# Two-layer decoder trunk on one core: norm factors spread by products, later norm sums, and another order in the first mixer

## The chip, the core and the metric

The kernel runs on one core of one Trainium2 chip. The metric is the device time of one execution in microseconds (us); lower is better. Five engines work side by side and meet at semaphores: TensorE (PE in the profile, its weight loads PEld), VectorE (DVE), ScalarE (ACT), GpSimd (POOL) and SyncE (SP), which here only issues the loads of weights. TensorE writes to eight PSUM banks; everything else lies in SBUF.

## What is computed

```python
def reference(...):                        # x: (1, 256, 1024) float32, two layers
    h = x
    for layer in range(2):
        h = h + 0.5 * swiglu(rms_norm(h, ffn1_norm[layer]), ...)     # FFN of width 2816
        hn = rms_norm(h, mix_norm[layer])
        if layer % 2 == 0:
            h = h + ab_mixer(hn, ab_w_in[0], ab_v_norm[0], ab_w_spatial[0], ab_b_spatial[0], ab_w_out[0])
        else:
            h = h + c_mixer(hn, c_w_in[0], c_w_out[0])
        h = h + 0.5 * swiglu(rms_norm(h, ffn2_norm[layer]), ...)
    return rms_norm(h, final_norm)
```

- `rms_norm(x, g)` is `x * rsqrt(mean(x*x) + 1e-6) * g`, `swiglu` is `(silu(x @ w_gate) * (x @ w_up)) @ w_down`.
- `ab_mixer` projects `hn` to q, k, v of 8 heads of 64 (attention with three dilated windows, which for 256 positions is one causal attention with a count mask) and to u and v of 4 groups of 128: `gelu(u) * (tril(w_s) @ rms_norm(gelu(v)) + b_s)`. Both results, side by side, go through `ab_w_out`.
- `c_mixer` is causal attention of 16 heads of 64 (with 256 positions there is one block only), then `c_w_out`.

## The kernel before

**Layout.** The residual `X` lies transposed: 8 tiles of 128 features by 256 positions. All products are made in three passes, `mm3` (L224 to L226): each operand is split into a rounded part and a rest (names ending in h and l, or `whi` and `wlo`), and hi x hi, lo x hi, hi x lo are added in a PSUM bank.

**Weights.** `Stream` loads them in a fixed list of pieces of 1 MB or less (`raw`, three buffers, SP queue). Each piece is split by ScalarE (L105, `whi`) and VectorE (L106, `wlo`), in two halves of 128x1024, into one of four buffers. A piece's buffer comes free when TensorE has used it (`free`), and the next split follows. A piece marked `reset` has another layout: its first three row blocks are stored as halves elsewhere, and it is split in three cuts (128x384 twice, 128x1280).

**Norms.** The next phase begins on features that are not yet divided by the root of the mean square. `Next.pair` adds a phase's result to `X`, makes the operands `xTh`, `xTl`, and squares; `acc` (L283 to L289, VectorE) adds the squares. `sums` (L295) adds them over features with two products with a column of ones, VectorE adds epsilon (L297, `ms`), GpSimd takes the power -0.5 (L233, `rstd`). `spread` (L310 to L317) brings the factor of a position to all 128 partitions: ScalarE writes `wide`, the factor of each position along a row; TensorE transposes it in two steps of 128x128 (L313); ScalarE copies the bank to `row` and half of it to `half`. An FFN calls `sums` after its second tile and `spread` after its third.

**Mixers.** A tile of projected features is 24 matmuls of 256 columns (`tiles`, two to a piece). `token_block` makes 512 columns of v, positions in the partitions: four steps of 12 matmuls of 512 columns. After each step `Slots.step` runs the work entered for that slot: `scores` of one head (four matmuls; then the row maximum on VectorE, Exp on ScalarE, the scaling by 1/sum, which the first mixer does on ScalarE, L688, and the second on GpSimd, L690), `turn` (three transposes L698, split into `pth` on ScalarE and `ptl` on VectorE), `weighted` (six matmuls with v for a pair of heads, split into `mixh` and `mixl`), and in the first mixer `mixing` of one gating group (two FP32 products, L839, then VectorE and a split). `put_q`, `put_k`, `put_u`, `put_v`, `keep_g` take a bank away: q and k need `row` (VectorE), ScalarE and GpSimd; u and g need Gelu on ScalarE (L857, L822).

`first_tiles` makes the first two q tiles and the first two k tiles (slots 0 to 3) in four banks, calls `sums` between them and `spread` behind them, and then takes the four banks away.

The first mixer's order is q and k of heads 0 to 3, v (slots 4 to 7), g (8 to 11), u (12 to 15), q and k of heads 4 to 7 (16 to 19), then `project` (20 on), which takes the eight parts of the concatenated result in the order `MIX1`: gating groups first. The order of the instructions of each engine's queue comes from a scheduler that starts from this order; each engine runs its queue strictly in order. ScalarE reads its functions from a table; the program holds a load (`ACT_TABLE_LOAD`) wherever the next function is not in the loaded one. Copies and squares do not change it, while Exp, Gelu and Silu each do.

Of the kernel before, what the change touches and what calls it, by code (L numbers as in the profile page):

```python
# [10 lines left out]
F32 = mybir.dt.float32  # L11
F32R = mybir.dt.float32r
AF = mybir.ActivationFunctionType
ALU = mybir.AluOpType
# [3 lines left out]
NT = S // 128  # L18
KD = D // 128
# [4 lines left out]
SCALE = HD ** -0.5  # L24
# [118 lines left out]
def trunk(ctx: ExitStack, tc: tile.TileContext, a, out):  # L143
# [40 lines left out]
        for c in (0, 512):  # L184
            st.add(m[k * 128 : (k + 4) * 128, c : c + 512], 4, 512, SHIFT)

    MIX1, MIX2 = (4, 5, 6, 7, 0, 1, 2, 3), (0, 1, 2, 3, 4, 5, 6, 7)
    add_ffn(a["ffn1_w_gate"][0], a["ffn1_w_up"][0], a["ffn1_w_down"][0], again=(1, 3))
    wab = a["ab_w_in"][0]
    add_cols(wab, 0, 256)  # L190
    add_cols(wab, 512, 256, reset=RESET)
    add_cols(wab, 1024, 512)
    add_cols(wab, 2048, 512)
    for c, n in ((1536, RESET), (1792, 0), (256, RESET), (768, RESET)):
        add_cols(wab, c, 256, reset=n)
    add_mix(a["ab_w_out"][0], MIX1)
    add_ffn(a["ffn2_w_gate"][0], a["ffn2_w_up"][0], a["ffn2_w_down"][0])
    add_ffn(a["ffn1_w_gate"][1], a["ffn1_w_up"][1], a["ffn1_w_down"][1])
    wc = a["c_w_in"][0]
    for c in range(4):  # L200
        add_cols(wc, c * 256, 256, reset=RESET if c % 2 else 0)
        add_cols(wc, 1024 + c * 256, 256, reset=0 if c else RESET)
        if c % 2 == 0:
            add_cols(wc, 2048 + c * 256, 512)
    add_mix(a["c_w_out"][0], MIX2)
    add_ffn(a["ffn2_w_gate"][1], a["ffn2_w_up"][1], a["ffn2_w_down"][1], True, (2, 3, 7))


# [36 lines left out]
    class Next:  # L245
# [59 lines left out]
        def spread(self):  # L305

            y = norm["col"]
            b = wk.tile([128, NT, 128], F32, name="wide", bufs=1)
            for t in range(NT):
                nc.scalar.activation(b[:, t], ones, AF.Copy, scale=y[:, t : t + 1])  # L310
            p = bank()
            for t in range(NT):
                nc.tensor.transpose(p[:, t * 128 : (t + 1) * 128], b[:, t], ident)  # L313
# [435 lines left out]
            step()  # L749
        st.free()  # L750

    def first_tiles(put_q, put_k, step):

        ps4 = [bank() for _ in range(4)]
        w = st.take()
        for j, ks in LATE:
            tile_of(ps4[j], w, j, ks)
        for _ in range(2):
            step()
        st.free()  # L760
        nxt.sums()
        w = st.take()
        for j in range(2):
            tile_of(ps4[2 + j], w, j)
            step()
        nxt.spread()
        norm["score"] = wk.tile([128, NT], F32, name="score", bufs=1)
        nc.vector.tensor_scalar(norm["score"], norm["col"], -SCALE, None, op0=ALU.mult)
        for j in range(2):
            put_q(j, ps4[j])  # L770
            put_k(j, ps4[2 + j])
        st.free()


    def token_block(evict, step):
# [20 lines left out]
    def ab_mixer(phase):  # L796
        with tc.tile_pool(name="mp", bufs=1) as mp:
            mix = mix_tiles(mp)
            v = v_tiles(mp, 512)
            vn = mp.tile([128, NT, 512], F32, name="vn")  # L800
            uT = mp.tile([128, 4, S], F32, name="uT")
            put_q, put_k, scores, turn, weighted = make_attention(mp, slice(0, 384), 8, v, mix, nc.scalar)

            vgain = mp.tile([128, 512], F32, name="vgain")
            nc.scalar.dma_start(vgain, rows(a["ab_v_norm"][0], 512))
            wsp = mp.tile([128, 4, 128], F32, name="wsp")
            nc.scalar.dma_start(wsp, a["ab_w_spatial"][0].rearrange("g p q -> p g q"))
# [12 lines left out]
            def keep_g(t, p):  # L820
                g = mp.tile([128, 512], F32, name="gv")
                nc.scalar.activation(g, p, AF.Gelu_apprx_tanh, scale=norm["col"][:, t : t + 1])  # L822
                ss = wk.tile([128, 4], F32, name="ssg")
                for q in range(4):
                    nc.scalar.activation(vn[:, t, q * 128 : (q + 1) * 128], g[:, q * 128 : (q + 1) * 128], AF.Square,
                                         accum_out=ss[:, q : q + 1])
                m = wk.tile([128, 4], F32, name="msg")
                nc.vector.tensor_scalar(m, ss, 1.0 / 128, EPS, op0=ALU.mult, op1=ALU.add)
                y = wk.tile([128, 4], F32, name="rsg")
                rsqrt(y, m, 4)  # L830
                for q in range(4):
                    cs = slice(q * 128, (q + 1) * 128)
                    nc.vector.scalar_tensor_tensor(vn[:, t, cs], g[:, cs], y[:, q : q + 1], vgain[:, cs],
                                                   op0=ALU.mult, op1=ALU.mult)

            def mixing(g):
                p = bank()
                for t in range(NT):
                    nc.tensor.matmul(p[:, t * 128 : (t + 1) * 128], vn[:, t, g * 128 : (g + 1) * 128],  # L839
                                     wsT[:, g, :], start=True, stop=True)  # L840
# [12 lines left out]
            slots.at((13, 14, 24, 25), weighted)  # L853

            def put_u(i, p):
                nc.vector.tensor_mul(uT[:, i, :], p[:, :S], norm["row"])
                nc.scalar.activation(uT[:, i, :], uT[:, i, :], AF.Gelu_apprx_tanh)  # L857

            step = slots.step
            first_tiles(put_q, put_k, step)  # L860
            token_block(lambda t, p: put_v(v, t, p), step)
            token_block(keep_g, step)
            for put, c in ((put_u, 0), (put_u, 1), (put_q, 1), (put_k, 1)):
                tiles(put, c, step)
            project(mix, MIX1, phase, step)
            assert not slots.events


    def c_mixer(phase):
        with tc.tile_pool(name="mp", bufs=1) as mp:  # L870
            mix = mix_tiles(mp)
            v = v_tiles(mp, D)
            put_q, put_k, scores, turn, weighted = make_attention(mp, slice(384, 768), 16, v, mix, nc.gpsimd, True)

            slots = Slots()
            slots.at((5, 6, 7, 8, 12, 13, 14, 15, 16, 17, 18, 19, 24, 24, 25, 25), scores)
            slots.at((8, 9, 10, 11, 15, 16, 17, 18, 19, 20, 21, 22, 26, 26, 27, 27), turn)
            slots.at((11, 13, 18, 20, 22, 24, 28, 29), weighted)
            step = slots.step
            for c in range(4):  # L880
                if c:
                    tiles(put_q, c, step)
                    tiles(put_k, c, step)
                else:
                    first_tiles(put_q, put_k, step)
                if c % 2 == 0:
                    token_block(lambda t, p: put_v(v, t, p, c * 256), step)
            project(mix, MIX2, phase, step)
            assert not slots.events


# [46 lines left out]
```

## Time and profile before

| | before |
|---|---|
| time, median of 3 runs | 948.4 us (948.16 to 948.5) |
| profiled execution, its own time | 948.47 us |
| its span, first to last instruction | 946.7 us |
| granted TensorE clock, mean | 0.999 |
| instructions | 18120 |
| first mixer, first to last of its matmuls on TensorE | about 190 to 284.6 us |
| second mixer, the same | about 646 to 764 us |
| weights and inputs read | 172.65 MB |

How to read it: a busy share is that of the whole span. Matmuls overlap, so TensorE's busy share counts the time in which any of them is under way; what it loses is seen in the distance from one start to the next. In a list of groups, the last column is the idle time of the engine just ahead of these instructions, and who ended most of it. In a list of waits, the numbers are the total in us, how many, and the longest. In a timeline the first two numbers are the start and the duration in us. In a table of windows the columns are the window, its length, and the busy time (with the number of instructions) of PE, PEld, DVE, ACT and POOL, then the clock, the share of the DMA engines and GB/s.

### The profile page before, as it was taken

The numbers are of one execution on the slowest core, as the hardware profiler recorded it, in microseconds if no ns is written. First come the engines' busy times: TensorE is split into PE (matmuls) and PEld (weight loads), VectorE is DVE, ScalarE is ACT, GpSimd is POOL, SyncE is SP. The second block draws the span as 40 slices with busy tenths as digits, with TensorE's granted clock in tenths as the row PEclk, the third lists the DMA queues.
The fourth block names the chain that finished last, engine by engine and source line by source line (L and its number), as shares of the span: only waits on it lengthen the run. The fifth ranks groups of instructions, "written<-read, shape, count | busy, mean of one in ns | idle before, by whom it ended". The sixth has DMA issues, their size and how long they took to land.

```text
span 946.7 us, 18120 instructions
## 1 busy us (share of the span) xinstructions
PE 935.5 (99%) x7679; PEld 911.8 (96%) x7679; DVE 607.1 (64%) x865; ACT 506.8 (54%) x801; POOL 87.0 (9%) x112
## 2 busy tenths in 40 slices
PE   9999999999999999999999999999999999999997
PEld 9999999988999999999999999999999999999886
DVE  6856656677877665655665665567787766665543
ACT  6745444469675544544554444455786655544431
POOL 0000000030200000000000000003684200000000
PEclk9999999999999999999999999999999999999999
DMA  9966555665445666546656665656544476555521
GB/s 293 287 188 209 171 189 179 223 220 178 134 134 183 205 192 189 197 161 211 214 187 180 206 194 163 205 180 220 173 140 135 134 216 204 179 181 197 204 89 44
DMA packets 153537, 174.86 MB, mean 185 GB/s; under 512 B 3008, under 2 KB 142192, under 8 KB 153456
## 3 DMA queue, kind: packets, MB, share of 16 engines
q1 hardware_dynamic: 151888, 171.54, 56.6%
q10 hardware_dynamic: 1568, 2.17, 0.7%
q8 instruction: 60, 0.98, 0.4%
q14 instruction: 21, 0.17, 0.1%
HBM read 172.65 MB, written 1.05 MB: 183 GB/s over the span
## 4 chain that ended last, share of the span: by engine, by line
PE 66%; DVE 4%; ACT 3%; issue 1%; POOL 0%; POOLq 0%; ACTq 0%
PE bank L225 20%; PE bank L224 20%; PE bank L226 20%; DVE wlo L106 2%; PE bank L544 2%; PE bank L547 2%; PE bank L543 2%; ACT whi L105 1%; ACT pr L681 1%; PE bank L698 0%; DVE xTl L262 0%; PE bank L674 0%; PE bank L675 0%; DVE mixl L230 0%; ACT pr L688 0%
## 5 line engine op out<-in xcount | busy, mean ns | idle before, releaser
L105 ACT ACTIVATE whi<-raw 128x1024 fp32r<-128x1024 f32 (+4 forms) x350 | 331.3, 990 | 369.0 <-issue 285.7
L106 DVE TENSOR_TENSOR wlo<-raw,whi 128x1024 fp32r<-128x1024 f32 (+4 forms) x350 | 390.6, 1148 | 133.4 <-ACT whi L105 132.2
L224 PE MATMUL bank<-xTh,whi 128*128 128x256 f32 x1632 | 452.9, 278 | 0.0
L225 PE MATMUL bank<-xTl,whi 128*128 128x256 f32 x1632 | 451.6, 277 | 0.2 <-DVE xTl L262 0.2
L226 PE MATMUL bank<-xTh,wlo 128*128 128x256 f32 x1632 | 451.3, 277 | 0.2 <-DVE wlo L106 0.2
L225 PEld LDWEIGHTS bank<-xTl,whi 128*128 128x128 f32 x1632 | 306.5, 188 | 0.9 <-DVE xTl L262 0.8
L226 PEld LDWEIGHTS bank<-xTh,wlo 128*128 128x128 f32 x1632 | 306.4, 188 | 0.6 <-DVE wlo L106 0.6
L224 PEld LDWEIGHTS bank<-xTh,whi 128*128 128x128 f32 x1632 | 306.4, 188 | 0.1
L224 PE MATMUL bank<-hTh,whi 128*128 128x256 f32 x528 | 145.7, 276 | 0.0
L225 PE MATMUL bank<-hTl,whi 128*128 128x256 f32 x528 | 145.7, 276 | 0.0
L226 PE MATMUL bank<-hTh,wlo 128*128 128x256 f32 x528 | 145.7, 276 | 0.0
L224 PEld LDWEIGHTS bank<-hTh,whi 128*128 128x128 f32 x528 | 99.1, 188 | 0.0
L226 PEld LDWEIGHTS bank<-hTh,wlo 128*128 128x128 f32 x528 | 99.1, 188 | 0.0
L225 PEld LDWEIGHTS bank<-hTl,whi 128*128 128x128 f32 x528 | 99.1, 188 | 0.0
L486 DVE TENSOR_TENSOR hm<-gs,bank 128x512 f32<-128x512 f32 x44 | 30.1, 687 | 80.8 <-PE bank L226 80.5
L483 DVE TENSOR_TENSOR gs<-bank,row 128x512 f32<-128x512 f32 x44 | 30.0, 689 | 47.2 <-PE bank L226 47.2
L224 PE MATMUL bank<-mixh,whi 128*128 128x256 f32 x128 | 35.1, 280 | 0.0
L225 PE MATMUL bank<-mixl,whi 128*128 128x256 f32 x128 | 35.0, 277 | 0.0
L226 PE MATMUL bank<-mixh,wlo 128*128 128x256 f32 x128 | 34.9, 277 | 0.0
L626 POOL MEMSET zeros<- 128x256 f32 x2 | 0.6, 313 | 342.0 <-DVE x L273 342.0
L690 POOL TENSOR_SCALAR pr<-pr,rl 128x128 f32<-128x128 f32 (+1 forms) x32 | 30.2, 955 | 15.4 <-DVE rl L684 15.1
L230 DVE TENSOR_TENSOR hTl<-hm,hTh 128x512 fp32r<-128x512 f32 x44 | 30.1, 685 | 2.1 <-ACT hTh L229 2.1
(137 smaller groups left out, 881.0 us busy)
## 6 DMA issues: line engine op xcount, KB each, us to landing
raw<-in_ffn_w_gate SPq DMA_DIRECT2D x42, 1024.0 KB, 5.4
raw<-in_ffn_w_up SPq DMA_DIRECT2D x42, 1024.0 KB, 5.4
raw<-in_ffn_w_down SPq DMA_DIRECT2D x35, 1024.0 KB, 5.1
raw<-in_c_w_in SPq DMA_DIRECT2D x12, 1024.0 KB, 5.2
raw<-in_ab_w_in SPq DMA_DIRECT2D x10, 1024.0 KB, 5.1
raw<-in_ffn_w_down SPq DMA_DIRECT2D x12, 768.0 KB, 4.5
raw<-in_ab_w_out SPq DMA_DIRECT2D x4, 1024.0 KB, 4.9
raw<-in_c_w_out SPq DMA_DIRECT2D x4, 1024.0 KB, 4.9
```

Source lines behind the costliest of these rows:

```text
L105: nc.scalar.activation(hi, r, AF.Copy)
L106: nc.vector.tensor_sub(lo, r, hi.bitcast(F32))
L224: nc.tensor.matmul(p, sh, mh, start=start, stop=False)
L225: nc.tensor.matmul(p, sh, ml, start=False, stop=False)
L226: nc.tensor.matmul(p, sl, mh, start=False, stop=stop)
L230: nc.vector.tensor_sub(lo, src, hi.bitcast(F32))
L483: nc.vector.tensor_mul(g, both(pg), twice(norm["row"]))
L486: nc.vector.tensor_mul(hm, g, both(pu))
L543: nc.tensor.matmul(banks[t, h], sh, w[0][kw][:, cs], start=k == 0, stop=False)
L544: nc.tensor.matmul(banks[t, h], sh, w[1][kw][:, cs], start=False, stop=False)
L547: nc.tensor.matmul(banks[t, h], sl, w[0][kw][:, cs], start=False, stop=k == FT - 1)
L690: engine.tensor_scalar(pr[:, cs], pr[:, cs], rl[:, b : b + 1], None, op0=ALU.mult)
```

## The change

1. `spread`: the two transposes (L313) become ordinary FP32 products of the same operands, `wide` with the identity.
2. `first_tiles`, in both mixers: `sums` comes after the first k tile, not after the second q tile; `spread` and taking away the four banks become an event of slot 4, behind the first step of the v block.
3. First mixer: q and k of heads 4 to 7 come ahead of u. Scores, turns, weighted sums and gating groups get other slots; the projection takes its parts in natural order, attention first.
4. Second mixer: the first four heads' scores and turns are two slots later, the first two weighted sums at 13 and 14.
5. Three pieces of the first mixer and one of the second lose their `reset` layout; one keeps it.

```diff
-    MIX1, MIX2 = (4, 5, 6, 7, 0, 1, 2, 3), (0, 1, 2, 3, 4, 5, 6, 7)
+    MIX = tuple(range(KD))
...
-    add_cols(wab, 512, 256, reset=RESET)
+    add_cols(wab, 512, 256)
     add_cols(wab, 1024, 512)
     add_cols(wab, 2048, 512)
-    for c, n in ((1536, RESET), (1792, 0), (256, RESET), (768, RESET)):
+    for c, n in ((256, RESET), (768, 0), (1536, 0), (1792, 0)):
         add_cols(wab, c, 256, reset=n)
...
-        add_cols(wc, 1024 + c * 256, 256, reset=0 if c else RESET)
+        add_cols(wc, 1024 + c * 256, 256, reset=0)
...
-                nc.tensor.transpose(p[:, t * 128 : (t + 1) * 128], b[:, t], ident)
+                nc.tensor.matmul(p[:, t * 128 : (t + 1) * 128], b[:, t], ident, start=True, stop=True)
...
-    def first_tiles(put_q, put_k, step):
+    def first_tiles(slots, put_q, put_k):
...
         for _ in range(2):
-            step()
+            slots.step()
         st.free()
-        nxt.sums()
         w = st.take()
         for j in range(2):
             tile_of(ps4[2 + j], w, j)
-            step()
-        nxt.spread()
-        norm["score"] = wk.tile([128, NT], F32, name="score", bufs=1)
-        nc.vector.tensor_scalar(norm["score"], norm["col"], -SCALE, None, op0=ALU.mult)
-        for j in range(2):
-            put_q(j, ps4[j])
-            put_k(j, ps4[2 + j])
+            if j == 0:
+                nxt.sums()
+            slots.step()
         st.free()
+
+        def put(_):
+            nxt.spread()
+            norm["score"] = wk.tile([128, NT], F32, name="score", bufs=1)
+            nc.vector.tensor_scalar(norm["score"], norm["col"], -SCALE, None, op0=ALU.mult)
+            for j in range(2):
+                put_q(j, ps4[j])
+                put_k(j, ps4[2 + j])
+
+        slots.at((4,), put)
...
-            slots.at((15, 16, 17, 18), mixing)
-            slots.at((6, 7, 8, 9, 20, 20, 21, 21), scores)
-            slots.at((9, 10, 11, 12, 22, 22, 23, 23), turn)
-            slots.at((13, 14, 24, 25), weighted)
+            slots.at((19, 20, 21, 22), mixing)
+            slots.at((7, 8, 9, 10, 16, 16, 17, 18), scores)
+            slots.at((10, 11, 12, 13, 18, 18, 19, 20), turn)
+            slots.at((13, 15, 20, 21), weighted)
...
-            for put, c in ((put_u, 0), (put_u, 1), (put_q, 1), (put_k, 1)):
+            for put, c in ((put_q, 1), (put_k, 1), (put_u, 0), (put_u, 1)):
                 tiles(put, c, step)
-            project(mix, MIX1, phase, step)
+            project(mix, MIX, phase, step)
...
-            slots.at((5, 6, 7, 8, 12, 13, 14, 15, 16, 17, 18, 19, 24, 24, 25, 25), scores)
-            slots.at((8, 9, 10, 11, 15, 16, 17, 18, 19, 20, 21, 22, 26, 26, 27, 27), turn)
-            slots.at((11, 13, 18, 20, 22, 24, 28, 29), weighted)
+            slots.at((7, 8, 9, 10, 12, 13, 14, 15, 16, 17, 18, 19, 24, 24, 25, 25), scores)
+            slots.at((10, 11, 12, 13, 15, 16, 17, 18, 19, 20, 21, 22, 26, 26, 27, 27), turn)
+            slots.at((13, 14, 18, 20, 22, 24, 28, 29), weighted)
```

More of the change, by code (lines that the diff above doesn't have):

```diff
@@ L190, in trunk @@
     add_cols(wab, 0, 256)
-    add_cols(wab, 512, 256, reset=RESET)
+    add_cols(wab, 512, 256)
     add_cols(wab, 1024, 512)
     add_cols(wab, 2048, 512)
-    for c, n in ((1536, RESET), (1792, 0), (256, RESET), (768, RESET)):
+    for c, n in ((256, RESET), (768, 0), (1536, 0), (1792, 0)):
         add_cols(wab, c, 256, reset=n)
-    add_mix(a["ab_w_out"][0], MIX1)
+    add_mix(a["ab_w_out"][0], MIX)
     add_ffn(a["ffn2_w_gate"][0], a["ffn2_w_up"][0], a["ffn2_w_down"][0])
@@ L201, in trunk @@
         add_cols(wc, c * 256, 256, reset=RESET if c % 2 else 0)
-        add_cols(wc, 1024 + c * 256, 256, reset=0 if c else RESET)
+        add_cols(wc, 1024 + c * 256, 256, reset=0)
         if c % 2 == 0:
             add_cols(wc, 2048 + c * 256, 512)
-    add_mix(a["c_w_out"][0], MIX2)
+    add_mix(a["c_w_out"][0], MIX)
     add_ffn(a["ffn2_w_gate"][1], a["ffn2_w_up"][1], a["ffn2_w_down"][1], True, (2, 3, 7))
@@ L859, in ab_mixer @@
             step = slots.step
-            first_tiles(put_q, put_k, step)
+            first_tiles(slots, put_q, put_k)
             token_block(lambda t, p: put_v(v, t, p), step)
             token_block(keep_g, step)
-            for put, c in ((put_u, 0), (put_u, 1), (put_q, 1), (put_k, 1)):
+            for put, c in ((put_q, 1), (put_k, 1), (put_u, 0), (put_u, 1)):
                 tiles(put, c, step)
-            project(mix, MIX1, phase, step)
+            project(mix, MIX, phase, step)
             assert not slots.events
@@ L884, in c_mixer @@
                 else:
-                    first_tiles(put_q, put_k, step)
+                    first_tiles(slots, put_q, put_k)
                 if c % 2 == 0:
                     token_block(lambda t, p: put_v(v, t, p, c * 256), step)
-            project(mix, MIX2, phase, step)
+            project(mix, MIX, phase, step)
             assert not slots.events
```

## The prediction, made before the changed kernel was run

> **What bounds the kernel now.** I read the page first: engine totals, then the chain that ended last.
>
> ```profile
> PE 935.5 (99%) x7679; PEld 911.8 (96%) x7679; DVE 607.1 (64%) x865; ACT 506.8 (54%) x801; POOL 87.0 (9%) x112
> PE 66%; DVE 4%; ACT 3%; issue 1%; POOL 0%; POOLq 0%; ACTq 0%
> ```
>
> TensorE is the clock of this kernel. Next, busy time by windows: a stretch inside an FFN, the two stretches of the first mixer from its last v block to the end of its projection, and the start of the FFN behind it.
>
> ```profile
> 30.00:180.00 150.00, 150.00 (x1326) 150.00 (x1325) 94.82 (x108) 72.83 (x90) 0.00 (x0) 1.00 0.63 201
> 226.00:262.00 36.00, 35.13 (x292) 34.14 (x291) 27.93 (x62) 25.10 (x55) 9.68 (x10) 1.00 0.44 147
> 262.00:284.00 22.00, 21.17 (x171) 19.79 (x171) 15.50 (x40) 17.45 (x45) 0.11 (x1) 1.00 0.46 144
> 284.00:296.00 12.00, 12.00 (x102) 11.84 (x102) 10.18 (x16) 7.00 (x12) 0.00 (x0) 1.00 0.52 160
> ```
>
> The FFN runs one 256-column matmul per 150/1326 = 0.113 us with no gap; ScalarE (the fourth busy number) is half idle there. In the mixer ScalarE is busy 25.1 of 36 us, then 17.5 of 22. So only the mixers leave TensorE anything to gain or lose. The waits of TensorE there, first mixer (190 to 285 us), then the longest of the second (640 to 770):
>
> ```profile
> PE bank L674 <- POOL k L662: 0.9, 2, 0.7
> PE bank L225 <- DVE ptl L230: 0.7, 1, 0.7
> PE bank L295 <- DVE acc L289: 0.6, 1, 0.6
> ...
> PE bank L295 <- DVE acc L289: 0.8, 1, 0.8
> ```
>
> A matmul shows 0.28 us but the next starts 0.11 later, so each wait costs its idle time plus 0.17: the norm sums (L295) cost 0.77 and 0.97 = 1.74; scores waiting for k and the weighted sum waiting for ptl cost 0.9 + 0.7 + 3 x 0.17 = 2.1.
>
> **Sums a tile later: -1.74.** Both sums now stand 24 matmuls (2.7 us) later, while acc was late by under 1 us. The wait goes; the four L295 passes stay. Next is spread, again 5.4 us of matmuls behind the sums, as before, and TensorE waited for nothing there.
>
> **Products for transposes: +1.4.** A spread before (two transposes), and an FP32 product of the same 128x128 shape (two products, L839, the nearest row):
>
> ```profile
> 302.07 0.38 PE L313 MATMUL bank<-ident,wide 128*128 128x128 f32 x2
> 302.20 0.36 PE L224 MATMUL bank<-xTh,whi 128*128 128x256 f32 x1
> 302.40 0.28 PE L225 MATMUL bank<-xTl,whi 128*128 128x256 f32 x1
> ...
> 244.48 0.60 PE L839 MATMUL bank<-wsT,vn 128*128 128x128 f32 x4
> 244.84 0.37 PE L224 MATMUL bank<-xTh,whi 128*128 128x256 f32 x1
> 245.05 0.28 PE L225 MATMUL bank<-xTl,whi 128*128 128x256 f32 x1
> ```
>
> Two transposes are two records, two products four. From their first record to the second matmul behind them: 302.40 - 302.07 = 0.33 against 245.05 - 244.48 = 0.57. So +0.24 on TensorE for each of six spreads, nothing hides it: 1.4 (0.24 in the first mixer, 1.2 elsewhere).
>
> **q and k ahead of u: the table loads.** With the old order, heads 4 to 7 were scored after all Gelu work of u; the old ScalarE stream has three table loads in this mixer. The changed program's ScalarE stream, which can be listed without running it, has ten: scores now fall between gv (L822) and u (L857), so Gelu and Exp alternate. Rows of ScalarE in the first mixer give the price of each step, start to start:
>
> ```profile
> 212.96 1.28 ACT L681 ACT_TABLE_LOAD   x1
> 214.25 0.40 ACT L681 ACTIVATE pr<-pr,nm 128x128 f32<-128x128 f32 x1
> ...
> 215.75 1.04 ACT L105 ACTIVATE whi<-raw 128x1024 fp32r<-128x1024 f32 x1
> 216.70 0.79 ACT L688 ACTIVATE pr<-pr,rl 128x128 f32<-128x128 f32 x2
> 217.39 0.50 ACT L681 ACTIVATE pr<-pr,nm 128x256 f32<-128x256 f32 x1
> ...
> 227.38 0.69 ACT L822 ACTIVATE gv<-bank,rstd 128x512 f32<-128x512 f32 x1
> 227.97 0.52 ACT L105 ACTIVATE whi<-raw 128x384 fp32r<-128x384 f32 x1
> ...
> 230.33 0.30 ACT L825 ACTIVATE vn<-gv 128x128 f32<-128x128 f32 x1
> ...
> 231.50 0.48 ACT L229 ACTIVATE pth<-bank 128x384 fp32r<-128x384 f32 x1
> ...
> 236.31 0.40 ACT L857 ACTIVATE uT<-uT 128x256 f32<-128x256 f32 x1
> 236.62 0.36 ACT L229 ACTIVATE mixh<-bank 64x256 fp32r<-64x256 f32 x1
> ...
> 248.03 0.85 ACT L650 ACTIVATE q<-qk 64x256 fp32r<-64x256 f32 x2 [1.45 <-DVE qk L637]
> ...
> 266.81 0.39 ACT L681 ACTIVATE pr<-pr,nm 128x128 f32<-128x128 f32 x1
> ...
> 267.69 0.39 ACT L681 ACTIVATE pr<-pr,nm 128x128 f32<-128x128 f32 x1
> ...
> 270.07 0.87 ACT L229 ACTIVATE pth<-bank 128x384 fp32r<-128x384 f32 x2
> 270.82 2.01 ACT L105 ACTIVATE whi<-raw 128x1024 fp32r<-128x1024 f32 x2
> ```
>
> A load takes 1.29 and nothing overlaps it: it starts as vth ends and Exp follows at once. The Trainium skill, "ScalarE: Activation LUTs", What ACT_TABLE_LOAD costs, states about 1.28 for the load and as much again for a drain, 2.66 a switch; the row shows the load and no gap behind it, so the sum goes by 1.29.
>
> From the load ahead of gv to the split of mix[2] (what matmuls of the projection's third k need) the changed ScalarE stream holds: 9 loads x 1.29 = 11.6; Exp of 5 heads x 0.88 = 4.4; their scaling 5 x 0.69 = 3.5; 12 weight halves x 0.95 = 11.4; 2 gv x 0.59 = 1.2; their squares 2 x 1.17 = 2.3; 8 pth x 0.38 = 3.0; 8 q and k halves x 0.43 = 3.4; 4 u x 0.31 = 1.2; 8 mixh x about 0.3 = 2.4. Sum 44.4 us.
>
> When does it start? After the scaling of head 2. Before:
>
> ```profile
> 216.90 0.39 PE L226 MATMUL bank<-whi,xTl 128*128 128x512 f32 x1
> 217.12 0.28 PE L674 MATMUL bank<-k,q 128*128 128x256 f32 x1
> ...
> 284.63 0.28 PE L224 MATMUL bank<-xTh,whi 128*128 128x256 f32 x1
> ...
> 222.08 0.51 ACT L105 ACTIVATE whi<-raw 128x384 fp32r<-128x384 f32 x1
> ```
>
> Head 2 was scored at 217.12 and scaled by 222.08, 4.96 later. Now it is scored one slot later (12 x 0.22 = 2.7), behind the four transposes of the spatial weights (0.45), with one product more (0.24) and without the wait (-0.77): 219.7, scaled by 224.7. With ScalarE never idle, mix[2] is split at 224.7 + 44.4 = 269.1; DVE's mixl adds 0.4: 269.5. Behind it the projection still has two steps of 24 matmuls, four of 12 and a last 48: 144 x 0.113 = 16.3, so the next FFN starts at 285.8, against 284.63 before. TensorE alone would be there at 284.63 - 2.1 - 0.77 + 0.24 - 16.3 = 265.7. So even this floor costs 3.8 of waiting, more than the 2.1 it replaces: the mixer ends 1.2 later, sums, product and old stalls included.
>
> ScalarE will not be busy without a gap. Following both streams, it waits for DVE before the second gv (its buffer is still read) and before the first u, which on DVE stands behind two weight halves and two mixl: 2.0 together. On DVE two more weight halves stand ahead of ptl of head 7, at 1.2 each (row below): +2.4 before the last weighted sum, which on TensorE stands ahead of all that is left of the projection.
>
> ```profile
> 244.58 1.21 DVE L106 TENSOR_TENSOR wlo<-raw,whi 128x1024 fp32r<-128x1024 f32 x1
> ...
> L857 ACT ACTIVATE uT<-uT 128x256 f32<-128x256 f32 x4 | 1.6, 408 | 2.9 <-DVE uT L856 2.9
> L229 ACT ACTIVATE mixh<-bank 64x256 fp32r<-64x256 f32 x8 | 3.0, 376 | 3.1 <-DVE mixl L230 2.6 <-PE bank L226 0.5
> ```
>
> Bounds for the idle time: nothing, or what u and mixh waited before, 2.9 + 3.1 = 6.0; I take 2.0, a third, since the fuller queue leaves later entries ready.
>
> **The rest.** Fewer RESET layouts: TensorE's pace is 12/102 = 0.118 in the window from 284, against 0.113; some 200 matmuls of k and u could keep it, 0 to 0.9 us; it is left out of the sum and kept for the range. In the second mixer the first heads are scored two slots later, with the same three slots from scores to turn; its table loads stay as they are. No DMA is added; the SP queue's order of weights changes with the tiles and its loads keep three buffers ahead.
>
> **Sum.** First mixer 1.2 + 2.0 + 2.4 = +5.6; second mixer's sums -0.97; five other products +1.2: +5.8. The profiled execution took 948.47 (span 946.7 and 1.77 around it), 0.07 above the median 948.4: 954.3.
>
> **Rivals.** *The loads fall into idle time (faster).* ScalarE idled 58 - 42.6 = 15.4 us in the two windows, more than seven loads' 9.0. If mix[2] is split by 265.7, the point from which it decides, nothing new waits: -1.74 - 2.1 + 1.4 = -2.4, 946.1. Against it: that needs 3.8 less than a gapless queue. *Only the floor (no change).* DVE keeps up and ScalarE never idles: 1.2 - 0.97 + 1.2 = +1.4, 949.9. *A switch costs more.* If each of the seven added loads stalls ScalarE for as long again, 7 x 1.29 = 9.0 on top: 963. The Trainium skill's section above has this as its rule; the row at 214.25 speaks against it. *The change doesn't do what it says:* the sums still wait, because two weight halves on DVE now stand ahead of ms (L297); then spread would wait in their place, at most 0.77 and 0.97: 954.3 + 1.74 = 956.
>
> **How the numbers follow.** A measurement of this kernel can tell about 0.2%, 1.9 us, from no change. Queue as worked out (950.4 to 957.5, which takes idle time from almost nothing to 5.2): 0.73, the sums still waiting included. Floor or near it: 0.16. Loads hidden: 0.07. Costlier switches: 0.04. Slower 0.77, same 0.16, faster 0.07. The range 949.5 to 957.5 leaves out the costlier switches, the hidden loads and the lower part of the floor case.
>
> **What the profile after would show.** Fifteen table loads against 8; L313 with 24 records instead of 12; no wait of L295; in the first mixer waits of TensorE for ptl and for mixh or mixl (from ScalarE's queue) of 6 to 9 us in all, with ScalarE above 85% busy from 226 us to the end of attention; the second mixer about 0.7 shorter. Wrong would be: TensorE waits under 3 us in the first mixer (the loads are hidden), or loads with gaps behind them.

## Result: 1.0% slower, where 0.6% was forecast

| | before | after |
|---|---|---|
| median of 7 runs each | 948.4 us | 958.25 us |
| lowest and highest | 947.79, 954.89 | 956.44, 963.38 |
| profiled execution, its span | 948.47, 946.7 | 962.7, 961.0 |

The ratio is 1.0102, 95% interval 1.0064 to 1.0141. The forecast was 954.3 with a range of 949.5 to 957.5; the result lies above it.

The times of both kernels fall into two groups some 6 us apart. Of the seven executions before, two took 954.2 and 954.9 and five 947.8 to 948.5; of the seven after, three took 962.7 to 963.4 and four 956.4 to 958.3. The profiled execution after is one of the longer ones. Where a median of the shorter group is given below, it says so: 948.2 before (five runs), 957.3 after (four runs), so +9.1.

The head of the page of the changed kernel, busy time and the shares of the chain that ended last:

```profile
PE 946.0 (98%) x7691; PEld 922.4 (96%) x7691; DVE 608.0 (63%) x861; ACT 515.6 (54%) x804; POOL 88.7 (9%) x112
PE 90%; ACT 3%; issue 2%; DVE 2%; DMA 1%; POOL 1%; SPq 0%; POOLq 0%; ACTq 0%
```

TensorE's 12 more matmuls are the products. TensorE still carries the chain; totals don't show where 14 us of span went. Windows do. The columns are as in the prediction: window, length, busy time of PE, PEld, DVE, ACT, POOL (with instructions), granted clock, DMA share, GB/s. Each mixer runs from its first matmul to the first of the FFN behind it; by that the second mixer before ends at 757.04, where the table further up has some 764. The kernel before, first and second mixer:

```profile
190.10:284.63 94.53, 92.24 (x684) 85.99 (x683) 72.02 (x153) 70.82 (x158) 19.87 (x25) 1.00 0.51 167
646.04:757.04 111.00, 110.04 (x840) 104.51 (x839) 85.83 (x191) 81.92 (x183) 61.47 (x74) 1.00 0.48 154
```

The changed kernel, a stretch of the first FFN, the first mixer, the third FFN, the second mixer and the last FFN:

```profile
30.00:180.00 150.00, 150.00 (x1276) 150.00 (x1275) 89.94 (x98) 69.21 (x85) 0.00 (x0) 1.00 0.61 194
196.29:298.91 102.62, 95.91 (x686) 89.44 (x685) 72.99 (x151) 80.26 (x163) 19.39 (x25) 0.97 0.48 154
...
479.84:660.84 181.00, 181.00 (x1595) 180.88 (x1593) 110.54 (x124) 84.76 (x107) 0.70 (x1) 1.00 0.61 192
...
660.84:771.05 110.21, 110.03 (x842) 104.70 (x841) 85.81 (x191) 81.62 (x183) 63.62 (x74) 1.00 0.48 156
771.05:954.28 183.23, 182.99 (x1358) 172.78 (x1356) 103.67 (x117) 82.08 (x107) 1.28 (x2) 1.00 0.52 167
```

Three things are to be read here. The first mixer takes 102.62 against 94.53, +8.1, with ScalarE busy 9.4 us more and a mean clock of 0.97. The second takes 110.21 against 111.00, -0.8. And the first FFN, which the change hardly touches, runs one matmul per 150/1276 = 0.118 us in this execution, against 150/1326 = 0.113 before: its matmuls end 6.2 us later, at 196.29 against 190.10. The other three FFNs take 0.75 more together; in sum that is the 14 us.

TensorE's waits over the whole run, those of over 0.2 us outside the start (in all, times, longest):

```profile
PE bank L224 <- ACT pth L229: 3.6, 2, 2.9
PE bank L225 <- DVE ptl L230: 2.8, 1, 2.8
```

Both waits of L295 are gone, and all that is left is in the first mixer. pth is made on ScalarE. ptl, of 2.8, stood in VectorE's queue behind the gate's vn, which waited for the root of the gate's norm (GpSimd), made from ScalarE's squares of the second gv:

```profile
247.30 1.36 DVE L838 SCALAR_TENSOR_TENSOR vn<-gv,rsg,vgain 128x128 f32<-128x128 f32 x4 [1.19 <-POOL rsg L233]
...
249.62 0.56 DVE L230 TENSOR_TENSOR ptl<-bank,pth 128x384 fp32r<-128x384 f32 x1
```

ScalarE's loads in that mixer, its u, and TensorE's products of `spread`:

```profile
L681 ACT ACT_TABLE_LOAD x5 | 6.4, 1283 | 0.1
L862 ACT ACT_TABLE_LOAD x3 | 3.8, 1283 | 0.1
L827 ACT ACT_TABLE_LOAD x2 | 2.6, 1283 | 1.0 <-DVE vn L838 1.0
L862 ACT ACTIVATE uT<-uT 128x256 f32<-128x256 f32 x4 | 1.7, 418 | 2.4 <-DVE uT L861 2.3
...
L313 PE MATMUL bank<-ident,wide x24: 270/275/377, 25.7 to 789.1; 128*128 128x128 f32 x24
```

Ten loads for three, at 1.28 each, and 24 records of L313 for 12. ScalarE's queue, in order of time (start, duration, instruction, idle time ahead of it):

```profile
230.35 1.28 ACT L827 ACT_TABLE_LOAD   x1
231.64 0.69 ACT L827 ACTIVATE gv<-bank,rstd 128x512 f32<-128x512 f32 x1
...
242.44 1.28 ACT L827 ACT_TABLE_LOAD   x1 [0.95 <-DVE vn L838]
...
256.18 0.42 ACT L862 ACTIVATE uT<-uT 128x256 f32<-128x256 f32 x1 [2.33 <-DVE uT L861]
...
281.26 0.38 ACT L229 ACTIVATE mixh<-bank 64x256 fp32r<-64x256 f32 x1
```

From the load at 230.35 to the end of the split of mix[2] at 281.64 (281.26 + 0.38) are 51.3 us. The prediction had 44.4 of work and 2.0 of waiting for it.

The trace after also holds something that no row before shows. Windows around the two long waits:

```profile
248.00:251.64 3.64, 1.41 (x10) 1.31 (x10) 3.58 (x8) 2.63 (x6) 1.51 (x2) 1.00 0.00 0
251.64:255.05 3.41, 3.41 (x18) 3.41 (x17) 3.32 (x6) 2.15 (x5) 1.90 (x2) 0.50 0.54 199
...
276.00:278.93 2.93, 0.25 (x3) 0.06 (x1) 2.77 (x6) 2.93 (x6) 0.00 (x0) 1.00 0.00 0
278.93:282.34 3.41, 3.21 (x10) 2.71 (x11) 3.38 (x6) 2.68 (x5) 0.00 (x0) 0.50 0.32 80
```

Behind each long wait the granted clock is 0.50 for 3.41 us. The Trainium skill, "TensorE: Matmul & The Clock Gate", What's actually happening, states half clock after an idle window of about 3.4 us, in windows of 3413 ns; the trace agrees with the length (3.41), and here it came with 2.9 us of idle time in the second case.

### The profile page after: what moved, and what is told of

Its sections match the earlier page's. It is cut to its first block, busy times and chain, and to the rows that moved or that the text cites. A ratio compares the mean times of both kernels' runs of the same rounds, so it can differ in the third digit from the quotient of the medians.

```text
span 961.0 us, 18146 instructions
## 1 busy us (share of the span) xinstructions
PE 946.0 (98%) x7691; PEld 922.4 (96%) x7691; DVE 608.0 (63%) x861; ACT 515.6 (54%) x804; POOL 88.7 (9%) x112
## 4 chain that ended last, share of the span: by engine, by line
PE 90%; ACT 3%; issue 2%; DVE 2%; DMA 1%; POOL 1%; SPq 0%; POOLq 0%; ACTq 0%
PE bank L225 27%; PE bank L224 27%; PE bank L226 27%; PE bank L547 2%; PE bank L544 2%; PE bank L543 2%; DMA raw<-in_ffn_w_up 1%; ACT whi L105 1%; DVE wlo L106 1%; PE bank L698 0%; ACT pr L681 0%; ACT L862 0%; PE bank L675 0%; PE bank L674 0%; PE bank L313 0%
## 5 line engine op out<-in xcount | busy, mean ns | idle before, releaser
L105 ACT ACTIVATE whi<-raw 128x1024 fp32r<-128x1024 f32 (+3 forms) x346 | 330.6, 999 | 379.9 <-issue 301.2
L106 DVE TENSOR_TENSOR wlo<-raw,whi 128x1024 fp32r<-128x1024 f32 (+3 forms) x346 | 389.3, 1158 | 132.4 <-ACT whi L105 131.2
L233 POOL TENSOR_TENSOR rstd<-ms,half_neg 128x2 f32<-128x2 f32 x6 | 5.1, 853 | 282.8 <-DVE ms L297 266.0
```

Source lines behind the costliest of these rows:

```text
L105: nc.scalar.activation(hi, r, AF.Copy)
L106: nc.vector.tensor_sub(lo, r, hi.bitcast(F32))
L233: nc.gpsimd.tensor_tensor(y, m, half_neg[:, :n], op=ALU.pow)
```

## Experiments

The theory: in the first mixer, loads and order fill ScalarE's queue, and TensorE's end there follows from it; the sums gain 0.8 in each mixer; the products cost 0.2 each; the pace of an FFN is drawn anew in each execution and belongs to neither kernel. The rivals are in each expectation. Stage lengths come from the profiled execution, from first matmul to first matmul.

### The order alone

```diff
-            for put, c in ((put_u, 0), (put_u, 1), (put_q, 1), (put_k, 1)):
+            for put, c in ((put_q, 1), (put_k, 1), (put_u, 0), (put_u, 1)):
```

with natural order of the projection, the layouts following their tiles, and slots `mixing` 19 to 22, `scores` (6, 7, 8, 9, 16, 16, 17, 18), `turn` (9 to 12, 18, 18, 19, 20), `weighted` (13, 15, 20, 21).

> The kernel before with one part of the change alone: q and k of heads 4 to 7 ahead of u, with the slots that go with it; sums, transposes and RESET layouts stay as before. ScalarE's stream then holds 13 table loads (8 in the first mixer, 3 before). Theory A (the order is the cost: ScalarE's queue grows by table loads, the weighted sum of head 7 and the projection wait for it): the first mixer takes +6 to +9 us against its 94.5 in the profile before, the other stages nothing, the time about 955 to 957. Theory B (the order is harmless, since ScalarE idled enough, and the loss of the changed kernel comes from the sums, the products or the missing RESET layouts): the first mixer within 1 us of 94.5, the time 946 to 949.

Measured: median 957.64 of 10 runs (shorter group 957.6, nine runs). First and second mixer:

```profile
196.49:299.53 103.04, 96.14 (x684) 89.19 (x683) 73.13 (x153) 77.83 (x163) 17.33 (x25) 0.97 0.47 153
660.48:771.50 111.02, 110.06 (x840) 104.52 (x839) 85.99 (x191) 81.97 (x183) 61.54 (x74) 1.00 0.47 154
```

+8.5 in the first mixer, nothing in the second: the order alone makes the whole loss. The time is 0.6 above theory A's. The profiled execution (963.14) is one with a first FFN at 0.118, as in the changed kernel.

### The sums alone

The changed `first_tiles` in the kernel before, with `scores` (7, 8, 9, 10, 20, ...), `turn` (10 to 13, 22, ...), `weighted` (14, 15, 24, 25) in the first mixer and the changed slots in the second.

> The kernel before with another part alone: the norm's sums and spread a tile later in both mixers, with the slots of the first heads that this moves; u stays ahead of q and k, transposes and RESET layouts stay. Because the first heads are scored later, two more table loads fall between them (10 against 8). Theory A (the sums are the gain of the change): the waits of L295 go, second mixer -0.8 to -1.0, first mixer -0.8 with up to 2 x 1.29 of loads against it if nothing hides them, so -0.8 to +1.8; the time 946.5 to 949.5. Theory B (the sums are what costs, because spread or the scores then wait in their place): both mixers at least 1 us longer, the time above 950.5.

Measured: median 947.95 of 10 runs (shorter group 947.9, against 948.4 of the kernel before on the same chip).

```profile
189.99:284.52 94.53, 92.28 (x684) 86.19 (x683) 71.28 (x153) 73.11 (x159) 20.47 (x25) 1.00 0.52 167
652.64:762.81 110.17, 109.99 (x840) 104.62 (x839) 85.78 (x191) 81.67 (x183) 63.52 (x74) 1.00 0.48 155
```

The second mixer gains 0.83; the first gains nothing. ScalarE is busy 2.3 us more there (its two added loads are 2.6), and TensorE's longest wait for k (L674 for L662) is 1.2 where it was 0.7, which takes most of the 0.77 back.

### No table switches

```diff
-                nc.scalar.activation(g, p, AF.Gelu_apprx_tanh, scale=norm["col"][:, t : t + 1])
+                nc.scalar.activation(g, p, AF.Exp, scale=norm["col"][:, t : t + 1])
...
-                nc.scalar.activation(uT[:, i, :], uT[:, i, :], AF.Gelu_apprx_tanh)
+                nc.scalar.activation(uT[:, i, :], uT[:, i, :], AF.Exp)
```

> The changed kernel with Exp in place of Gelu for u and the gate of the first mixer, which changes that part of the computation: the same number of ACTIVATE instructions of the same shapes, but ScalarE keeps one table there (6 loads in all, 15 in the changed kernel). Theory A (the added loads fill ScalarE's queue, and the waits of TensorE and the lower clock behind them follow from that): the first mixer takes 93 to 95.5 us, against 102.6 in the profile after, and the time is about 7 to 9 us under that of the changed kernel. Theory B (the loads are a side matter; the longer stay of weights, pth and ptl in the queues comes from the order of the work itself): the first mixer keeps at least 100 us.

and u alone (the second of the two edits):

> The changed kernel with Exp in place of Gelu for u alone, which changes that part of the computation; the gate keeps Gelu. ScalarE then has 5 table loads in the first mixer, between the 10 of the changed kernel and the 1 of the version without Gelu (95.6 us). Theory A (every load on ScalarE's queue there is on the path until TensorE becomes the bound): 5 x 1.28 = 6.4 less than 102.6, so 96 to 97.5. Theory B (only a few loads cost, those that alternate with gv ahead of the long wait for ptl): 100 or more.

Measured: medians 949.5 (4 runs) and 950.67 (10 runs). The first mixer without Gelu, and with Exp for u alone:

```profile
189.94:285.51 95.57, 92.30 (x686) 86.31 (x685) 72.49 (x151) 68.44 (x154) 17.94 (x25) 1.00 0.52 165
```

```profile
190.06:288.00 97.94, 94.00 (x686) 88.55 (x685) 72.97 (x151) 73.57 (x158) 17.82 (x25) 0.97 0.50 161
```

Ten loads take 102.62, five 97.94, one 95.57. The first five taken away give back 4.68 (0.94 each of 1.28), the next four 2.37 (0.59 each). So a load is mostly on the path while ScalarE is the bound, and less as TensorE becomes it. Theory A holds, its upper bounds missed by 0.07 and 0.44. Even without a switch, this order with later sums takes 1.0 more than before.

### Transposes put back in the changed kernel

```diff
-                nc.tensor.matmul(p[:, t * 128 : (t + 1) * 128], b[:, t], ident, start=True, stop=True)
+                nc.tensor.transpose(p[:, t * 128 : (t + 1) * 128], b[:, t], ident)
```

> The changed kernel with the transposes put back in the six spreads, everything else as changed. Theory A (each spread by products costs 0.24 on TensorE, and nothing hides it): -0.24 in each FFN behind the first and -0.24 in each mixer, 1.4 in all, which is less than a comparison of whole times can tell and is to be read from the stage lengths of the profile: the two middle FFNs -0.5 of 361.9, the last FFN -0.2 of 183.2. Theory B (a product in FP32 is no dearer than a transpose): these stages within 0.1 us of the changed kernel. No theory lets the first mixer's 102.6 fall by more than 1.

Measured: median 956.3 of 10 runs (shorter group 956.2, against 957.3). Third and last FFN:

```profile
480.89:661.43 180.54, 180.54 (x1592) 180.42 (x1591) 110.54 (x124) 84.77 (x107) 0.70 (x1) 1.00 0.61 193
771.44:954.45 183.01, 182.77 (x1356) 172.58 (x1354) 103.56 (x117) 82.06 (x107) 1.28 (x2) 1.00 0.52 167
```

-0.46 and -0.22 against the changed kernel. Over all profiles but that of the version with added RESET layouts (below), the last FFN takes 183.00 or 183.01 with transposes (once 183.21) and 183.23 with products, to the start of its last matmul. The third takes 180.52 to 180.54 (once 180.78) and 180.75 or 180.76; the 181.00 of the changed kernel stands alone, so half of the -0.46 is not the transposes'. That is 0.22 for a spread, theory A. In the first mixer, where ScalarE sets the end, it can't be seen: 103.98 here, 1.4 longer than with products. In that profile the first half clock sets in before the same wait of 2.8 is over, and lasts twice as long:

```profile
248.95:255.78 6.83, 5.84 (x25) 5.65 (x26) 6.09 (x10) 3.58 (x7) 2.43 (x4) 0.50 0.43 153
```

ScalarE then waits for TensorE ahead of a mixh, here and, as the second row, in the changed kernel:

```profile
251.84 0.38 ACT L229 ACTIVATE mixh<-bank 64x256 fp32r<-64x256 f32 x1 [1.22 <-PE bank L226]
...
251.37 0.38 ACT L229 ACTIVATE mixh<-bank 64x256 fp32r<-64x256 f32 x1 [0.45 <-PE bank L226]
```

### The weighted sum two slots later

```diff
-            slots.at((13, 15, 20, 21), weighted)
+            slots.at((13, 17, 20, 21), weighted)
```

> The changed kernel with the weighted sum of heads 2 and 3 two slots later (slot 17 for 15), so that TensorE has 48 matmuls, 5.3 us, of other work where it waited 0.7 and 2.8 us in a row. Theory A (TensorE's idle time there counts twice, as idle time and as 3.4 us at half clock behind it, while ScalarE's queue behind stays as long as before): the half clock of the stretch from 251 us goes; since ScalarE's later entries (pth of head 7) come when they did, most of the 3.5 us of waiting moves to that place, and the first mixer is 1 to 3 us shorter than 102.6. Theory B (only ScalarE's queue counts): the first mixer stays within 0.5 of 102.6. Theory C (the early wait was the whole loss): the first mixer falls below 98.

Measured: median 956.63 of 4 runs. First mixer, and TensorE's longest waits:

```profile
190.23:293.37 103.14, 96.35 (x686) 88.89 (x685) 73.45 (x151) 80.49 (x163) 19.58 (x25) 0.97 0.47 153
```

```profile
PE bank L224 <- ACT pth L229: 2.9, 1, 2.9
PE bank L698 <- ACT pr L688: 2.3, 2, 2.1
```

The wait for ptl and the half clock behind it are gone; a wait of 2.1 for the probabilities takes their place and brings no half clock; behind the later one, of 2.9, the clock is low for twice as long, and the mixer is 0.5 longer, just beyond theory B's bound. It is B all the same: ScalarE ends the split of mix[2] 84.9 behind the mixer's first matmul, 85.3 in the changed kernel, so the end moves with ScalarE's queue and not with TensorE's order.

### Filling TensorE's idle time

```diff
+            def filled(p):
+                if p % 2:
+                    f = bank()
+                    for _ in range(20):
+                        nc.tensor.transpose(f[:, :128], ident, ident)
+                weighted(p)
+
-            slots.at((13, 15, 20, 21), weighted)
+            slots.at((13, 15, 20, 21), filled)
```

> The changed kernel with 20 transposes of the identity into a spare bank ahead of the weighted sums of heads 2, 3 and of heads 6, 7: 2.2 us each of extra work for TensorE at the two places where it waits longest. Theory A (the clock halves when TensorE has idled over about 3 us, and for that alone): the waits shrink by what the transposes take, no half clock is granted, and the first mixer is 2 to 3.5 us shorter than 102.6, though TensorE does more. Theory B (the half clock has another cause, or costs nothing): the half clock stays, and the first mixer is as long or up to 2 us longer.

Measured: median 956.8 of 4 runs. First mixer, and TensorE's longest waits:

```profile
190.00:293.06 103.06, 98.11 (x726) 91.44 (x725) 73.35 (x151) 80.58 (x164) 19.57 (x25) 1.00 0.47 153
```

```profile
PE bank L698 <- ACT pr L688: 2.2, 2, 1.5
PE bank L225 <- DVE ptl L230: 1.9, 2, 1.6
```

Neither theory as a whole. The longest single wait is now 1.6 and the clock 1.00 throughout, so idle time is what halves it (A). But the mixer is no shorter: TensorE does 40 transposes more and loses no half clock, and ScalarE still ends the split of mix[2] where it did, 275.29 - 190.00 = 85.3 behind the mixer's first matmul, as in the changed kernel (281.64 - 196.29):

```profile
274.91 0.38 ACT L229 ACTIVATE mixh<-bank 64x256 fp32r<-64x256 f32 x1
```

So the half clock of the changed kernel came from the waits and didn't lengthen ScalarE's queue. Behind the split TensorE's end is 0.5 later than in the changed kernel. That the half clock is free is not shown: where it lasts 6.83 and holds up a mixh (transposes put back, above), the mixer is longer.

### Only the gain: the sums 12 matmuls later

In `first_tiles` of the kernel before; spread, scores and loads stay in their place:

```diff
-        nxt.sums()
         w = st.take()
         for j in range(2):
-            tile_of(ps4[2 + j], w, j)
+            if j == 0:
+                tile_of(ps4[2], w, 0, range(4))
+                nxt.sums()
+                tile_of(ps4[2], w, 0, range(4, KD))
+            else:
+                tile_of(ps4[3], w, 1)
             step()
```

> The kernel before with the sums of both mixers only 12 matmuls later (inside the next tile, not behind it) and all else in its place: spread, scores, table loads (8), transposes. Theory A (the gain of the sums needs only the 0.6 to 0.8 us by which acc was late, and no later spread): both waits of L295 go, spread does not wait, first mixer -0.8 and second mixer -1.0, and executions with all FFNs at the faster pace take 946.5 to 947. Theory B (ms stands behind two weight halves of DVE, so spread waits in the sums' place): a new wait of 0.5 to 1 us at L313, and no gain.

and this in the first mixer, with the changed `first_tiles` and slots in the second:

> The kernel before with the sums 12 matmuls later in the first mixer, and a whole tile later, spread with them, in the second mixer, where all heads use one table: a version that takes the gain of the sums in both places and none of the rest. Theory A (the stage lengths add up): first mixer 93.9, second 110.0, the rest as before; executions with every FFN at the faster pace take 946.4 to 946.9, against 948.2. Theory B (the gain of one mixer is given back by a wait behind it): 947.5 or more.

Measured: the first, median 947.0 of 12 runs (shorter group 946.95 of ten, the kernel before on the same chip 948.25); the second, median 946.83 of 12 (shorter group 946.8 of ten, before 948.3). Mixers of the first, then of the second:

```profile
189.87:283.74 93.87, 92.24 (x685) 86.36 (x683) 72.05 (x153) 70.85 (x158) 19.85 (x25) 1.00 0.52 168
645.16:755.62 110.46, 110.28 (x840) 104.69 (x839) 85.79 (x191) 82.05 (x183) 61.34 (x74) 1.00 0.48 155
```

```profile
189.38:283.48 94.10, 92.47 (x684) 86.65 (x683) 72.25 (x153) 71.05 (x158) 19.84 (x25) 1.00 0.52 168
650.81:760.99 110.18, 110.00 (x841) 104.61 (x839) 85.83 (x191) 81.66 (x183) 63.55 (x74) 1.00 0.48 155
```

Theory A for the waits: both of L295 are gone, and neither mixer has a new one at L313 (theory B). The gain is smaller than forecast: 0.66 and 0.54 in the first version; with spread later too the second mixer gains 0.82, and the first, of the same code, 0.43 in that profile. Why the first version gains only 0.54 in the second mixer stays open. Both versions lie under both kernels by their shorter groups, by 1.3 and 1.5 against the kernel before. Over all runs, longer ones included, the second one's ratio is 0.9981 (0.9961 to 1.0001), and the first's 0.9999 (0.9984 to 1.0014), whose two runs at 953.3 and 953.6 met none of that kind in the kernel before there.

### The pace of the FFNs

Two more profiles of the kernel before:

> The kernel before, unchanged, for a second profile. Its executions fall into two groups, about 948 and about 954.5 us. Theory A (a whole FFN runs at the slower matmul pace of 0.118 in some executions, as the first FFN does in the profile after, whatever the kernel): if this execution lies at 954, one of its FFNs is 6 to 7 us longer than in the first profile, with nothing else changed; if it lies at 948, all five FFNs are at 0.113. Theory B (the pace of the first FFN belongs to the change): every FFN here runs at 0.113, and a longer execution loses its time elsewhere.

> The kernel before, unchanged, for a third profile, with the same question: if this execution lies near 954, theory A has one FFN 6 to 7 us longer at the matmul pace of 0.118 and no other stage changed; theory B has every FFN at 0.113 and the time lost elsewhere. Near 948 it says nothing.

They took 947.91 and 948.24, so the question stayed open for that kernel itself: no execution of it near 954 was profiled. (The kernel has four FFNs.) Other kernels answered in part. In the versions with the order alone and with transposes put back (profiled executions of 963.14 and 962.84) the first FFN ran at the slower pace, as in the changed kernel. The version with the sums alone (profiled execution 954.26) and the last one above (952.43) both had a slow second FFN behind a fast first. Windows of the sums alone, within the first and second FFN:

```profile
30.00:180.00 150.00, 150.00 (x1326) 150.00 (x1325) 94.81 (x107) 72.73 (x90) 0.00 (x0) 1.00 0.63 201
310.00:460.00 150.00, 150.00 (x1276) 150.00 (x1275) 88.65 (x99) 67.59 (x84) 0.00 (x0) 1.00 0.58 184
```

The clock is 1.00 in both. So the pace doesn't belong to one FFN or to the change: a whole FFN runs at 0.118 in some executions, exactly one in each of these five profiles. How often is not alike everywhere. Of the kernel before, 20 of 25 executions lay near 954.5 on chip 14, and 0 of 17 and 2 of 28 on chip 11. Nor is it the chip alone: of the versions with the order alone, the sums alone, no Gelu and the transposes put back, run on chip 14 too, 4 of 34 executions were of the longer kind. Then more RESET layouts in the kernel before:

```diff
-    def add_ffn(wg, wu, wd, last=False, again=(2, 3)):
+    def add_ffn(wg, wu, wd, last=False, again=(2, 3, 5, 7, 9, 11)):
```

and so in the first FFN, (1, 3, 5, 7, 9, 11), and the last.

> The kernel before with the RESET layout in four more weight tiles of each FFN (from the fifth to the eleventh, every other one; the last FFN gets three more). Theory A (in executions of about 954 us one FFN stays at the slower pace of 0.118 because its first two RESET tiles didn't end it; each further RESET tile is another chance): executions above 953 become rare or the longest lie 1 to 5 us lower, while those at 948 stay within 0.3. Theory B (the slower pace doesn't depend on these layouts): the same share of executions near 954.5 as the kernel before shows on this chip. If the kernel before shows none there, this says nothing.

Measured: median 954.42 of 12 runs (951.72 to 958.98) against 948.33, ratio 1.0061 (1.0041 to 1.0081). Theory A falls: the added layouts make it slower. Windows of its first FFN, behind the last layout, and of the last FFN, behind the last layout too:

```profile
75.00:180.00 105.00, 105.00 (x929) 105.00 (x928) 62.35 (x71) 48.18 (x60) 0.00 (x0) 1.00 0.59 191
...
830.00:885.00 55.00, 55.00 (x470) 55.00 (x469) 33.52 (x35) 25.18 (x30) 0.00 (x0) 1.00 0.57 188
```

The first FFN stays at 105/929 = 0.113 and the last at 55/470 = 0.117 to the end of its 256-column matmuls. Between the layouts of the first FFN, by the distance from one start to the next, stretches of 85 matmuls at the faster pace and of 91 to 101 at the slower one alternate. So a RESET layout can end the fast pace as well as begin it. What sets the pace at the start of an FFN stays open.

## Why the prediction was wrong where it was, and right where it was

**Right: the sign, the place and the mechanism.** Loads and order in ScalarE's queue, TensorE waiting for it in the first mixer: shown by the order alone (+8.5) and by the versions with fewer loads (-7.0 without switches). A load cost 1.28 with nothing behind it, so the rival of the costlier switch falls: it gave 963, and three runs lie there, but the one of them that was profiled got there by the pace of an FFN. The Trainium skill's 2.66 a switch ("ScalarE: Activation LUTs", What ACT_TABLE_LOAD costs) is not what this trace shows: the next instruction starts 1.29 behind the load (230.35 to 231.64).

**Right: the smaller terms.** The second mixer -0.79 for -0.97 and +0.24; products 0.22 for 0.24. ScalarE was to be busy above 85% to the end of attention, and was: 46.26 of 52 us, 89%:

```profile
230.00:282.00 52.00, 45.29 (x333) 42.28 (x332) 34.62 (x82) 46.26 (x98) 8.71 (x10) 0.94 0.32 105
```

TensorE waited 6.4 in all (6 to 9 forecast), though 3.6 of it for pth, 2.8 for ptl and nothing for mixh or mixl. The 2.8 came out of VectorE's queue and didn't count for the end: with the later weighted sum it is gone and the mixer is no shorter.

**Wrong: the size of the first mixer, +8.1 for +5.6.** These terms of the step "q and k ahead of u" make the difference of 2.5:
- The idle time of ScalarE: 2.0 taken, between 0 and 6.0. Measured 4.8: 0.95 ahead of the second gv, 2.33 ahead of the first u (the two places that were named), and 0.5, 0.5 and 0.6 ahead of two mixh and a scaling. +2.8. "A fuller queue leaves later entries ready" was the reason for a third of the bound, and it didn't hold.
- The queue's work: 44.4 taken, 51.3 - 4.8 = 46.5 measured. The counts were right, and loads, scalings, q and k came as priced. The rest was priced at the distance to a next instruction that overlaps the end of it; where a load or an idle stretch follows, the whole duration counts. From start to start that is +0.5 for the weight halves, +0.4 for Exp, +0.3 each for u, mixh and pth, +0.2 for squares. +2.0.
- The start: 34.1 behind the mixer's first matmul for 34.6, -0.5. From mix[2] to the next FFN: 17.3 for 16.7, +0.6.
- ptl of head 7, "+2.4 before the last weighted sum": it didn't add. TensorE's wait there (2.9) was for pth, from the same queue; it didn't wait for that ptl. -2.4.

The idle time alone was inside the stated bounds; 954.3 + 2.5 = 956.8 would have been the forecast with the measured terms, and the shorter group's median was 957.3. That the term for ptl, which was wrong, made up for half of the other two, was luck.

**Not seen: the pace.** In "the rest" the pace of 0.118 was seen in one window and priced at up to 0.9 us, for the matmuls of the mixer. It can hold for a whole FFN. Its 1584 matmuls (22 pieces of 48 and 528 of the down projection) times 0.0045 are 7.1 us; between the two profiles the mixer begins 6.2 later. It moved the median from 957.3, just inside the range of 949.5 to 957.5, to 958.25, beyond it. The two executions of the kernel before near 954 could not be known from its three runs.

**Not seen: the half clock.** It had no row before. In the changed kernel it didn't lengthen ScalarE's queue (the filler), and that it is free elsewhere is not shown.

**The sums.** -1.74 for both was forecast and 0.8 came, in the second mixer; in the first they are hidden under ScalarE's queue. With the old order they gain nothing there with two more loads, and 0.4 and 0.7 in two profiles where the loads stay as they were.

## What to carry to other kernels

When two functions of different tables alternate on an engine, count the loads in the new order of the queue, not in the code; here seven more loads of 1.28 and the order that brought them cost 8 us, on an engine that had been a quarter idle there (70.82 of 94.53 busy). When one engine's queue has become the bound of a stage, work that is moved or saved on another engine there shows nothing: filling the waits, ending the half clock and moving the weighted sum all left the mixer at 103. It can still show where the bound engine has to wait for the other, as with the longer half clock (104). A gain of under 1 us is worth taking by the smallest move that brings it, since a later neighbour can cost a table load.

## What the runs showed of the hardware

- TensorE's 256-column matmuls have two paces at the same granted clock, 0.113 and 0.118 us, which last for stretches of some 85 matmuls to almost a whole FFN of 1584; in the version with added RESET layouts the pace changed both ways between them, and what else changes it is open. An FFN at the second pace costs 6 us.
- Half clock (0.50) came in stretches of 3.41 us or twice that, and the length of a single wait doesn't decide it: with the later weighted sum there was none behind a wait of 2.1, and with the order alone there was one behind a wait of 1.4. How busy TensorE was in the 3.41 us ahead of it does sort all cases here. Take each trace in stretches of 3.41 us, in step with its half-clock stretches. At full clock, from 190 to 770 us of all profiles, those that half clock followed held at most 1.84 us of matmuls, and those that full clock followed at least 1.91; once halved, it stayed so behind stretches with 2.25 to 2.42 and ended behind those with 2.91 or more. Two stretches of the changed kernel (251.63 begins the first half clock), one of the order alone with the half clock behind it, and the longer half clock of the later weighted sum:

```profile
244.81:248.22 3.41, 1.91 (x14) 1.40 (x12) 1.82 (x7) 3.33 (x13) 2.06 (x3) 1.00 0.00 0
248.22:251.63 3.41, 1.40 (x9) 1.30 (x10) 3.35 (x7) 2.40 (x5) 1.51 (x2) 1.00 0.00 0
...
259.76:263.17 3.41, 1.84 (x12) 1.30 (x12) 1.80 (x11) 3.39 (x11) 0.00 (x0) 1.00 0.38 131
263.17:266.58 3.41, 3.41 (x18) 3.41 (x18) 0.17 (x1) 3.38 (x8) 0.00 (x0) 0.50 0.01 2
...
271.54:278.37 6.83, 5.74 (x22) 5.23 (x23) 6.74 (x12) 4.60 (x10) 0.00 (x0) 0.50 0.50 154
```

The Trainium skill, "TensorE: Matmul & The Clock Gate", Why this matters for your kernels, says no idle gaps over about 3 us between bursts; here shorter ones, of 2.8 and 2.9 us and of 1.4, were followed by half clock.
- A load of a table takes 1.28 us and the next instruction follows within 0.02.
